# A two-layer hybrid trunk: mixers traced in small woven steps, and one block transpose per RWKV level spread on GpSimd

## The chip, the cores and the metric

One Trainium2 chip, one core. The metric is the device time of one execution in microseconds (us), the median over runs of the kernel.

## What is computed

A two-layer decoder trunk on 256 tokens of width 1024, in float32. A layer runs three mixers on the normed input h, gates and sums them, projects the sum, and then runs a dense FFN (layer 0) or a top-2-of-8 expert layer (layer 1):

```python
for l in range(DEPTH):
    mod = silu(c) @ ada_w[l] + ada_b[l]
    h = rms_norm(x, norm_mix[l]) * (1 + sc_m) + sh_m
    proj = h @ w_in[l]
    y_rw, v_first = rwkv7_mixer(...)   # S = S*w + (S a) b + v k, y = S r, per head
    y_ssd = ssd_mixer(...)             # conv, chunked state-space scan, gated norm
    y_fox = fox_mixer(...)             # causal softmax with forget gates
    merged = g_rw*(y_rw @ proj_rw[l]) + g_ssd*(y_ssd @ proj_ssd[l]) + g_fox*(y_fox @ proj_fox[l])
    x = x + g_m * (merged @ w_out[l])
    x = x + g_f * (FFN or experts)(h')
```

The RWKV recurrence is done in chunks of 128 tokens, for which a triangular 128 x 128 matrix per head has to be inverted.

## The kernel before

Every large product is made from halves: `split_part` (L148 to L158) rounds a piece of raw weights to float32r on ScalarE (L156, `hi`) and subtracts that from the raw piece on VectorE (L157, `lo`), and `mm3` (L125) multiplies hi by hi, hi by lo and lo by hi. The text calls each such TensorE instruction with 256 columns a product; a split of 128 x 512 feeds 12 of them (4 k-tiles x 3). Raw weights come in pieces of up to 1 MB through a ring of 3 buffers, loaded on SP's queue (`load_raw`). `project_cols` projects up to 256 columns of `w_in` at a time (48 products for 256 columns), `project_rows` does the same with h as weights, `gates` and `merge` project the branch gates and the branch outputs, and `mod_next` loads and sums a piece of the next modulation.

The mixers of one layer are written as generators: `rwkv_half` (two halves of four heads, tokens r0, r1), `ssd_group` (four groups, s0 to s3), `fox_half` (f0, f1), `gates` (G) and `merge` (m0 to m2). The list `ORDER` says in which order their pieces, which run from one `yield` to the next, are traced. A half of RWKV has four pieces: the projections; the decays and the matrices `mats`; the inversion; the states. A scheduler then orders each engine's instructions by the order of tracing and by what it takes to be ready; each engine runs its own list strictly in order. Merging in `ORDER` comes at the end: RWKV, SSD, FoX.

The inversion goes over levels 0 to 5 for two chunks (ch) of 128 tokens. In a level GpSimd masks the matrices (`pool.tensor_tensor`, L629, into `am`), TensorE multiplies four 32-row blocks with `tls` (L631), VectorE transposes each 32 x 128 block of the result into the diagonal blocks of `bds` (L654, four per chunk and level), TensorE multiplies by `bds` (L658), VectorE adds (L661), TensorE transposes the sum (L131) and ScalarE copies it out as `c` (L671), from which the next level starts. `bds` is zeroed once per half by GpSimd (L637). Tiles of 128 x 512 come from a ring `u` of `NUNIT` = 15, tiles `c` from a ring of `NCOMP` = 6.

The rest of the program is not touched: the first norm, `project_out`, the FFN and the experts are traced as before.

Of the kernel before, what the change touches and what calls it, by code (L numbers as in the profile page):

```python
# [36 lines left out]
NUNIT, NSSD, NSPLIT, NRAW, NB8 = 15, 7, 5, 3, 4  # L37
NMOE, NSM = 5, 7
NPOOL = 4
NCOMP = 6  # L40
# [10 lines left out]
ORDER = [  # L51
    (
        "rw r0 r0 mo r0 r0 fx sd s0 s0 s0 s1 s1 s1 r1 r1 r1 r0 s2 mo s2 s2 f0 r1 r1 s3 mo G f0 mo G s3 s3 G "
        "f0 G m0 f1 m0 f1 m0 md md m1 md m0 m1 m1 md f1 md md md m1 m2 gm m2 md m2 m2"
    ).split(),
    (
        "rw r0 r0 mo r0 sd s0 s0 r0 r0 s0 s1 mo s1 s1 s2 r1 r1 G r1 s2 fx r1 G s2 r1 G s3 s3 mo f0 f0 s3 G m0 "
        "f0 m0 mo m0 m0 f1 md f1 m1 m1 md md md gm m1 md m1 f1 m2 m2 m2 md md md m2"
    ).split(),
# [4 lines left out]
def trunk(  # L64
# [312 lines left out]
    def stationary(raw, n, evac):  # L377

        ps = dbank()
        for q in range(0, n, P):  # L380
            m = min(P, n - q)
            o = ps[:m, q * 2:q * 2 + T]
            accumulate(o, raw[:, :, q:q + m], (hh, hl))
            evac(q // P, o)

    def project_cols(wsrc, c0, n, evac):
        for p0 in range(0, n, 256):
            w = min(256, n - p0)
# [47 lines left out]
    def stages(f):  # L436

        def start(*a):
            g = f(*a)
            return lambda: next(g, None)  # L440
        return start
# [17 lines left out]
    def rwkv(mx, l, prm, lora):  # L459
# [10 lines left out]
        project_cols(w_in[l], 1536, 288, lambda i, ps: shift(wa if i == 0 else gl[:ps.shape[0], i - 1, :], ps, 12 + i))  # L470
# [14 lines left out]
        return [y[:, 0], y[:, 1]], lambda jp: stages(rwkv_half)(mx, l, prm, lora, jp, shift, wa, gl, vd, vup, y)  # L485

    def rwkv_half(mx, l, prm, lora, jp, shift, wa, gl, vd, vup, y):
# [8 lines left out]
        for dst, g in ((k, 1), (r, 0), (v, 2)):  # L496
            project_cols(w_in[l], g * RW + jp * 256, 256, lambda i, ps: shift(dst[:, i, :], ps, 4 * g + 2 * jp + i))
# [37 lines left out]


# [19 lines left out]


# [17 lines left out]


# [4 lines left out]


# [5 lines left out]
        act.activation(vrow, ps, AF.Copy)  # L588
# [909 lines left out]
```

## Time and profile before

| what | value |
|---|---|
| median of 3 runs | 2234.21 us (2226.03 to 2235.48) |
| profiled execution | 2224.52 us, span 2222.8 us |
| TensorE (PE) busy, its weight loads (PEld) | 2115.0 us (95%), 1811.2 us (81%) |
| VectorE (DVE) | 1798.8 us (81%) |
| ScalarE (ACT) | 1386.1 us (62%) |
| GpSimd (POOL) | 152.1 us (7%) |

The span falls into the first norm (to about 35 us), the mixers of layer 0 (to 478 us), the output projection and the FFN (to 722 us, with the second norm), the mixers of layer 1 (to 1171 us) and the experts. In the page's 40 slices GpSimd is busy in the mixers alone, and DMA is below a half of its share there, while it is at nine tenths in the experts.

### The profile page before, as it was taken

Reading aid. Unit: us, or ns where it says so; the run is one execution under the profiler, and the core shown is the slowest. Engines: PE = TensorE matmul, PEld = TensorE weight load, DVE = VectorE, ACT = ScalarE, POOL = GpSimd, SP = SyncE. Lnnn points to the kernel's source line nnn. Section 1 sums busy time; section 2 is a strip of 40 time slices with the busy share of each in tenths; the row PEclk is TensorE's granted clock in tenths of the full one; section 3 lists DMA queues with packets and bytes.
Section 4 is the critical chain, followed back from the end, with each engine's and each line's share of the span. In section 5 each row is a group of like instructions: output and inputs, shape, how many; then the busy total and the mean of one; then the engine's idle time right before and its main releaser. Section 6 shows DMA issues by size and latency. Waiting matters only on the chain.

```text
span 2222.8 us, 35724 instructions
## 1 busy us (share of the span) xinstructions
PE 2115.0 (95%) x13489; PEld 1811.2 (81%) x13489; DVE 1798.8 (81%) x2822; ACT 1386.1 (62%) x2204; POOL 152.1 (7%) x180
## 2 busy tenths in 40 slices
PE   7899899999998889989998999999999999999998
PEld 4777789998997877868998788888888887888776
DVE  4977776777776797756768999999999989999887
ACT  3454455555454545434555877878878777878775
POOL 2211200000000031211002000000000000000000
PEclk9999999999999998988998999999999999999999
DMA  8423254667884533414556999999999999999994
GB/s 304 128 83 95 77 172 156 213 198 259 294 286 137 145 108 93 138 53 130 184 176 251 337 362 359 324 368 367 374 337 352 355 362 336 342 364 368 336 363 151
DMA packets 316101, 546.68 MB, mean 246 GB/s; under 512 B 11952, under 2 KB 143536, under 8 KB 315920
## 3 DMA queue, kind: packets, MB, share of 16 engines
q1 hardware_dynamic: 315920, 544.31, 71.1%
q8 instruction: 108, 1.77, 0.3%
q14 instruction: 73, 0.60, 0.1%
HBM read 543.22 MB, written 1.05 MB: 245 GB/s over the span
## 4 chain that ended last, share of the span: by engine, by line
PE 79%; DVE 13%; issue 3%; ACT 2%; DMA 2%; POOL 0%; SPq 0%; DVEq 0%; ACTq 0%; POOLq 0%
PE pd L122 37%; PE pm L122 33%; PE ps L122 7%; DVE lo L157 5%; PE pm L131 1%; DVE u L654 1%; DMA araw<-in_ada_w_dram 1%; PE ps L131 1%; ACT hi L156 1%; DMA b<-in_ada_w_dram 1%; DVE cu L802 1%; DVE xr L1257 1%; DVE u L225 0%; DMA raw<-in_moe_w_gu_dram 0%; DVE b L612 0%
## 5 line engine op out<-in xcount | busy, mean ns | idle before, releaser
L156 ACT ACTIVATE hi<-raw 128x1024 fp32r<-128x1024 f32 (+2 forms) x1201 | 1027.7, 870 | 522.4 <-PE pd L122 277.0
L157 DVE TENSOR_TENSOR lo<-raw,hi 128x1024 fp32r<-128x1024 f32 (+2 forms) x1197 | 1154.6, 990 | 211.6 <-ACT hi L156 189.8
L122 PE MATMUL pd<-hh,hi 128*128 128x256 f32 (+2 forms) x1208 | 352.7, 293 | 15.3 <-ACT hh L362 3.9
L122 PE MATMUL pd<-hh,lo 128*128 128x256 f32 (+2 forms) x1208 | 346.5, 287 | 0.0
L122 PE MATMUL pd<-hl,hi 128*128 128x256 f32 (+2 forms) x1208 | 345.7, 286 | 0.3
L122 PE MATMUL pm<-lo,hh 128*128 128x512 f32 x672 | 266.7, 397 | 3.0 <-DVE lo L157 2.8
L122 PE MATMUL pm<-hi,hh 128*128 128x512 f32 x672 | 266.9, 397 | 0.1
L122 PE MATMUL pm<-hi,hl 128*128 128x512 f32 x672 | 263.0, 392 | 0.0
L122 PEld LDWEIGHTS pd<-hh,hi 128*128 128x128 f32 (+2 forms) x1208 | 231.9, 192 | 28.3 <-issue 5.6
L122 PEld LDWEIGHTS pd<-hh,lo 128*128 128x128 f32 (+2 forms) x1208 | 231.5, 192 | 6.1 <-issue 3.9
L122 PEld LDWEIGHTS pd<-hl,hi 128*128 128x128 f32 (+2 forms) x1208 | 232.7, 193 | 4.3 <-issue 2.3
L122 PE MATMUL pd<-lo,hi 128*128 128x512 f32 x448 | 174.7, 390 | 0.0
L122 PE MATMUL pd<-hi,hi 128*128 128x512 f32 x448 | 170.9, 391 | 0.1
L122 PE MATMUL pd<-hi,lo 128*128 128x512 f32 x448 | 167.8, 389 | 0.0
L122 PEld LDWEIGHTS pm<-lo,hh 128*128 128x128 f32 x672 | 126.8, 189 | 32.1 <-DVE lo L157 5.5
L122 PEld LDWEIGHTS pm<-hi,hh 128*128 128x128 f32 x672 | 126.5, 188 | 29.3 <-ACT hi L156 1.4
L122 PEld LDWEIGHTS pm<-hi,hl 128*128 128x128 f32 x672 | 126.7, 189 | 26.5
L122 PE MATMUL pm<-hi,more 128*128 128x512 f32 x448 | 142.1, 392 | 0.0
L122 PEld LDWEIGHTS pd<-hi,hi 128*128 128x128 f32 x448 | 84.1, 188 | 18.4 <-ACT hi L405 0.5
L122 PEld LDWEIGHTS pd<-hi,lo 128*128 128x128 f32 x448 | 84.1, 188 | 17.8
L122 PEld LDWEIGHTS pd<-lo,hi 128*128 128x128 f32 x448 | 84.1, 188 | 17.6
L122 PEld LDWEIGHTS pm<-hi,more 128*128 128x128 f32 x448 | 84.1, 188 | 17.5 <-ACT hi L156 0.3
(423 smaller groups left out, 3467.0 us busy)
## 6 DMA issues: line engine op xcount, KB each, us to landing
raw<-in_moe_w_gu_dram SPq DMA_DIRECT2D x224, 1024.0 KB, 7.0
raw<-in_moe_w_down_dram SPq DMA_DIRECT2D x110, 1024.0 KB, 6.8
raw<-in_w_in_dram SPq DMA_DIRECT2D x66, 1024.0 KB, 5.4
araw<-in_ada_w_dram SPq DMA_DIRECT2D x68, 512.0 KB, 4.3
raw<-in_ffn_w_gu_dram SPq DMA_DIRECT2D x22, 1024.0 KB, 6.8
raw<-in_ffn_w_down_dram SPq DMA_DIRECT2D x11, 1024.0 KB, 6.5
raw<-in_w_in_dram SPq DMA_DIRECT2D x16, 512.0 KB, 5.1
raw<-in_proj_ssd_dram SPq DMA_DIRECT2D x8, 1024.0 KB, 5.2
```

Source lines behind the costliest of these rows:

```text
L122: pe.matmul(o, lhsT, rhs, start=start, stop=stop)
L131: pe.transpose(o, i, ident[:n, :n])
L156: act.activation(hi, raw, AF.Copy)
L157: minus.tensor_sub(lo, raw, hi.bitcast(F32))
L654: dve.transpose(blk(bds[ch], q)[:, odd, bcol(q)], by4(blk(pz, q))[:, odd, :])
L802: dve.scalar_tensor_tensor(cu[:, s:T], ps[:, 0:T - s], pph[:, w:w + 1], cu[:, s:T], op0=ALU.mult, op1=ALU.add)
L1257: dve.tensor_add(xr[:, t, hs], xr[:, t, hs], po)
```

## The change

- `ORDER` becomes a list of segments. A segment holds up to three streams, whose steps are woven evenly: step i of n stands at (i + 0.5) / n. `STEPS` is the number of steps of each stream (45 for a half of RWKV, 14 for an SSD group).
- Many `yield`s are added, so that a step is one 128-column projection, one half of a level, one part of a softmax. Both layers have one order.
- SSD's gates (G) are computed first and SSD is merged first (`ma`), beside FoX; RWKV (`mb`) and FoX (`mc`) follow.
- In each level one VectorE transpose takes the whole 128 x 128 result into a tile `c`, and GpSimd multiplies it, repeated four times, by a block-diagonal mask `bmask` into `bds`. The zeroing of `bds` goes.
- `NUNIT` 15 to 14, `NCOMP` 6 to 8. Pieces of the modulation are all loaded as in `mo`; the deep form `md` is no longer used in the mixers.

```diff
-NUNIT, NSSD, NSPLIT, NRAW, NB8 = 15, 7, 5, 3, 4
+NUNIT, NSSD, NSPLIT, NRAW, NB8 = 14, 7, 5, 3, 4
-NCOMP = 6
+NCOMP = 8
-ORDER = [
-    (
-        "rw r0 r0 mo r0 r0 fx sd s0 s0 s0 s1 s1 s1 r1 r1 r1 r0 s2 mo s2 s2 f0 r1 r1 s3 mo G f0 mo G s3 s3 G "
-        "f0 G m0 f1 m0 f1 m0 md md m1 md m0 m1 m1 md f1 md md md m1 m2 gm m2 md m2 m2"
-    ).split(),
...
+STEPS = dict(r=45, s=14, f=21, G=9, ma=9, mb=17, mc=17)
+ORDER = 2 * [
+    [
+        ["rw"], ["r0:7"], ["sd"],
+        ["r0:25", "s0. s1:4", "mo"],
+        ["r0:8", "s1. s2:4", "mo"],
+        ["r0.", "r1:7 s2:2", "mo"],
+        ["r1:25", "s2. s3. G:4", "mo"],
+        ["r1:8", "G. ma:4", "mo"],
+        ["r1.", "fx f0:8 ma:2"],
+        ["f0.", "ma. f1:7", "mo mo"],
+        ["f1.", "mb:8", "mo mo"],
+        ["mb.", "mo"], ["gm"], ["mc."],
+    ],
 ]
...
         for ch in range(2):
             bds[ch] = unit(mx, 4, P)
-            pool.memset(bds[ch], 0.0)
...
             for ch in range(2):
                 pz = level(ch, lv, tls[ch])
-                for q in range(4):
-                    dve.transpose(blk(bds[ch], q)[:, odd, bcol(q)], by4(blk(pz, q))[:, odd, :])
+                ct = sq128()
+                dve.transpose(ct, pz)
+                pool.tensor_tensor(bds[ch].rearrange("p n (q c) -> p n q c", q=4)[:, odd],
+                                   by4(ct)[:, odd, :].unsqueeze(2).broadcast_to([P, len(range(4)[odd]), 4, 32]),
+                                   by4(bmask).unsqueeze(1).broadcast_to([P, len(range(4)[odd]), 4, 32]), op=ALU.mult)
+            yield
...
+                    b = (1, 0, 2)["abc".index(step[1])]
+                    return merge(mx, l, prm, b, made["merged"], made["y"][b], (proj_rw, proj_ssd, proj_fox)[b][l], (4, 8, 4)[b], b == 1)
...
+            for segment in ORDER[l]:
+                streams = [steps(stream) for stream in segment]
+                for _, _, name in sorted(((i + 0.5) / len(x), k, name) for k, x in enumerate(streams) for i, name in enumerate(x)):
+                    assert take(name), (name, counts, taken)
```

The order on ScalarE in layer 0, second half of RWKV, at the copies of the levels (`c<-pm`, two per level, one for each chunk); `hi<-raw` is the rounding that feeds 12 products, `s` and `ysh` are SSD's. Before, from the second copy of level 1 to the first of level 4:

```order
L671 ACTIVATE c_2418<-pm_2416 128x128
L847 ACTIVATE s_2848<-s_2848 128x512
L847 ACTIVATE s_2849<-s_2849 128x512
L671 ACTIVATE c_2458<-pm_2456 128x128
L671 ACTIVATE c_2462<-pm_2460 128x128
L671 ACTIVATE c_2502<-pm_2500 128x128
L671 ACTIVATE c_2506<-pm_2504 128x128
L872 ACTIVATE s_2969<-s_2878 128x512
L671 ACTIVATE c_2546<-pm_2544 128x128
```

and now, from the second copy of level 2 to the first of level 3 alone:

```order
L694 ACTIVATE c_3046<-pm_3044 128x128
L163 ACTIVATE hi_3695<-raw_3630 128x512
L163 ACTIVATE hi_3727<-raw_3724 128x512
L1000 ACTIVATE b_716_3233<-pd_3513,pph_234 128x256
L163 ACTIVATE hi_3743<-raw_3724 128x512
L163 ACTIVATE hi_3773<-raw_3724 128x512
L163 ACTIVATE hi_3789<-raw_3724 128x512
L694 ACTIVATE c_3159<-pm_3157 128x128
```

Where copies of two levels stood one behind the other, five splits of the SSD gates now stand between them.

The order on GpSimd in the same half: `u<-b,ztm` is the mask product of a level (`ztm_340` is level 2, `ztm_351` level 3, `ztm_362` level 4, `ztm_375` level 5; the two `b` are the two chunks), `u<-c,bmask` the new spread (`u_2886` for chunk 0, `u_2889` for chunk 1), `sm` a power for a norm:

```order
L648 TENSOR_TENSOR u_3087<-b_588_2730,ztm_351 128x512
L648 TENSOR_TENSOR u_3097<-b_607_2831,ztm_351 128x512
L648 TENSOR_TENSOR u_3172<-b_588_2730,ztm_362 128x512
L674 TENSOR_TENSOR u_2886<-c_2997,bmask 128x512
L674 TENSOR_TENSOR u_2889<-c_3007,bmask 128x512
L141 TENSOR_TENSOR sm_3193<-sm_3192,mhalf 128x2
L648 TENSOR_TENSOR u_3182<-b_607_2831,ztm_362 128x512
L648 TENSOR_TENSOR u_3270<-b_588_2730,ztm_375 128x512
L674 TENSOR_TENSOR u_2886<-c_3094,bmask 128x512
L674 TENSOR_TENSOR u_2889<-c_3104,bmask 128x512
```

Before, GpSimd had the mask products alone here; now the spread of level 2 stands behind the mask products of levels 3 and 4, and that of level 3 behind those of levels 4 and 5 and behind a power that waits for SSD.

## Rows read from the trace of the kernel before

**Rows 1.** Windows, stretches of both mixers: length, busy us by engine, PEclk, DMA share, GB/s

```profile
core 0: us, PE busy (x) PEld busy (x) DVE busy (x) ACT busy (x) POOL busy (x), PEclk, DMA share, GB/s
44.60:71.50 26.90, 26.10 (x209) 23.93 (x209) 24.08 (x91) 17.34 (x41) 0.00 (x0) 1.00 0.42 114
71.50:253.30 181.80, 158.23 (x1378) 133.00 (x1382) 142.36 (x326) 79.50 (x194) 46.77 (x55) 0.93 0.31 91
253.30:478.20 224.90, 222.80 (x1868) 205.49 (x1864) 158.07 (x310) 125.98 (x275) 11.15 (x10) 0.99 0.56 176
722.30:763.00 40.70, 38.55 (x313) 35.55 (x314) 29.81 (x93) 26.01 (x56) 0.00 (x0) 1.00 0.55 154
763.00:970.00 207.00, 184.64 (x1560) 155.25 (x1563) 168.24 (x367) 97.42 (x234) 49.45 (x53) 0.93 0.36 106
970.00:1171.00 201.00, 195.72 (x1604) 177.94 (x1596) 127.50 (x247) 105.24 (x226) 12.46 (x14) 0.94 0.47 147
```

**Rows 2.** Windows, the four stretches of levels 1 to 4, in order of time

```profile
108.00:140.00 32.00, 26.60 (x289) 21.04 (x284) 26.04 (x72) 13.62 (x39) 8.27 (x12) 0.89 0.35 113
224.40:253.30 28.90, 23.59 (x252) 17.64 (x248) 21.39 (x61) 10.20 (x33) 12.15 (x17) 0.89 0.15 38
795.60:833.20 37.60, 33.95 (x341) 28.09 (x341) 33.85 (x85) 15.56 (x35) 9.35 (x13) 0.86 0.29 86
945.40:970.00 24.60, 18.35 (x207) 13.91 (x211) 19.15 (x56) 8.37 (x29) 7.20 (x10) 0.93 0.15 45
```

**Rows 3.** Timeline of PE (start, length, idle before): products after a wait, and in a dense stretch

```profile
79.77 0.51 PE L122 MATMUL pd<-hh,hi 128*128 128x256 f32 x1 [2.96 <-DVE vfirst L468]
80.08 0.42 PE L122 MATMUL pd<-hl,hi 128*128 128x256 f32 x1
80.29 0.41 PE L122 MATMUL pd<-hh,lo 128*128 128x256 f32 x1
80.50 0.41 PE L122 MATMUL pd<-hh,hi 128*128 128x256 f32 x1
...
83.28 0.30 PE L122 MATMUL pd<-hl,hi 128*128 128x256 f32 x1
...
476.73 0.28 PE L122 MATMUL pd<-hi,hh 128*128 128x256 f32 x1
476.84 0.28 PE L122 MATMUL pd<-lo,hh 128*128 128x256 f32 x1
476.95 0.28 PE L122 MATMUL ps<-hi,hh 128*128 128x256 f32 x1
```

**Rows 4.** Lines by form: busy us, mean ns of one, idle before

```profile
L157 DVE TENSOR_TENSOR lo<-raw,hi 128x512 fp32r<-128x512 f32 x524 | 364.6, 703 | 150.2 <-ACT hi L156 142.8 <-PE pd L122 3.3 <-PE pm L131 0.5
L629 POOL TENSOR_TENSOR u<-b,ztm 128x512 f32<-128x512 f32 x48 | 59.9, 1265 | 104.5 <-PE pm L122 63.2 <-DVE b L612 41.2
L654 DVE STREAM_TRANSPOSE u<-pm 32x128 f32<-32x128 f32 x128 | 39.9, 312 | 14.1 <-PE pm L122 11.7
L654 DVE STREAM_TRANSPOSE u<-pm 32x64 f32<-32x64 f32 x32 | 7.9, 246 | 1.6 <-PE pm L122 1.0
```

**Rows 5.** Timeline of POOL in layer 0, mask products

```profile
97.47 8.06 POOL L629 TENSOR_TENSOR u<-b,ztm 128x512 f32<-128x512 f32 x6 [3.35 <-DVE b L612]
108.81 2.27 POOL L629 TENSOR_TENSOR u<-b,ztm 128x512 f32<-128x512 f32 x2 [3.28 <-PE pm L122]
```

**Rows 6.** Timeline of DVE beside them

```profile
97.67 1.50 DVE L225 SCALAR_TENSOR_TENSOR u<-araw,silc,u 128x512 f32<-128x512 f32 x1
99.10 0.72 DVE L612 COPY_PREDICATED b<-mmask,pm 128x512 f32<-128x512 uint8 x1
...
101.54 1.65 DVE L225 SCALAR_TENSOR_TENSOR u<-araw,silc,u 128x512 f32<-128x512 f32 x1
103.12 1.39 DVE L805 SCALAR_TENSOR_TENSOR xb<-zt,cu 128x256 f32<-128x256 f32 x1
104.42 1.65 DVE L157 TENSOR_TENSOR lo<-raw,hi 128x512 fp32r<-128x512 f32 x1
106.00 0.74 DVE L225 SCALAR_TENSOR_TENSOR u<-araw,silc,u 128x512 f32<-128x512 f32 x1
...
109.06 2.60 DVE L654 STREAM_TRANSPOSE u<-pm 32x128 f32<-32x128 f32 x8
...
113.55 0.43 DVE L805 SCALAR_TENSOR_TENSOR xb<-zt,cu 128x256 f32<-128x256 f32 x1 [0.59 <-ACT zt L804]
```

**Rows 7.** Waits, 71.5 to 253.3 us: total, times, longest

```profile
ACT hi L156 <- PE pd L122: 41.5, 32, 6.1
POOL u L629 <- PE pm L122: 31.2, 9, 6.9
...
PE pm L122 <- DVE u L654: 8.4, 9, 1.7
```

More of the change, by code (lines that the diff above doesn't have):

```diff
@@ L388, in project_cols @@
             w = min(256, n - p0)
-            stationary(load_raw(rows(wsrc, 0, D, c0 + p0, w), KD, w), w, lambda i, ps: evac(p0 // P + i, ps))
+            yield from stationary(load_raw(rows(wsrc, 0, D, c0 + p0, w), KD, w), w, lambda i, ps, i0=p0 // P: evac(i0 + i, ps))
     def project_rows(wsrc, c0, y):
@@ L434, in pair, with whole @@
         return keep(a, [P, KD, T], F32R), keep(b, [P, KD, T], F32R)
[L436 to L441, printed above, removed]
+    def whole(g):
+        while True:
+            try:
+                next(g)
+            except StopIteration as e:
+                return e.value
     def hblock(hb):
@@ L1003, in project_out @@
             qs = slice((q % 2) * 256, (q % 2) * 256 + 256)
-            ps = project_rows(w_out[l], q * 256, (mh, ml))
+            ps = whole(project_rows(w_out[l], q * 256, (mh, ml)))
             for t in range(2):
@@ L1391, in trunk, with steps @@
                     gm = keep("vfirst", [P, 2, 512]) if l == 1 else mx("u2", [P, 2, 512])
[L1392 to L1405 removed]
+                    made["gm"] = [gm[:, 0], gm[:, 1]]
+                    mod_row(lambda: unit(mx, 4, P), l, 2, 0.5, made["gm"])
+                else:
+                    if token not in run:
+                        run[token] = part(token)
+                    if run[token] is None:
+                        return False
+                    counts[token] = counts.get(token, 0) + 1
+                    if next(run[token], done) is done:
+                        run[token] = None
+                return True
+            taken = {}
+            def steps(stream):
+                names = []
+                for word in stream.split():
+                    name, _, n = word.rstrip(".").partition(":")
+                    n = STEPS[name if name in STEPS else name[0]] - taken.get(name, 0) if word[-1] == "." else int(n or 1)
+                    taken[name] = taken.get(name, 0) + n
+                    names += [name] * n
+                return names
+            for segment in ORDER[l]:
+                streams = [steps(stream) for stream in segment]
+                for _, _, name in sorted(((i + 0.5) / len(x), k, name) for k, x in enumerate(streams) for i, name in enumerate(x)):
+                    assert take(name), (name, counts, taken)
+            assert not any(run.values()), [k for k in run if run[k]]
+            merged, gm = made["merged"], made["gm"]
             dump(f"merged{l}", merged)
```

110 lines of the change are left out of this document (64 added, 46 removed).

## The prediction, made before the change was run

> **What bounds the kernel now.** I read the page's busy shares first, then the windows by stage, then the order, and then the lines, waits and timelines of the mixers. TensorE is 95% busy over the span, so only what PE loses counts, and the order says where to look: outside the mixers the instructions of FFN and experts stand as they did. The two mixers take 44.6 to 478.2 us and 722.3 to 1171 us; I split each at the first key norm of RWKV's half 0 and at the last level of half 1 [rows 1]. The middle stretch is where PE is not fed: in 71.5 to 253.3 us it is busy 158.2 of 181.8 us at a mean granted clock of 0.93, in 763 to 970 us 184.6 of 207 us at 0.93. The merges behind are dense: 222.8 of 224.9 us in layer 0. So products stand in a queue at the end of the mixer while PE idles in its middle. The worst part is the levels: four of them take 24.6 to 37.6 us, and PE is busy 74 to 90% of it, with small matmuls [rows 2]. A level is a chain PE, DVE, PE, DVE, PE, ACT, so it cannot hurry; what can be done is to put products between.
>
> The clock makes a gap dearer than it is. After PE had waited 2.96 us, products followed each other at 0.213 us (80.29 to 80.50), down to 83.28; in a dense stretch at 0.113 us [rows 3]. That is 1.2 against 2.4 GHz. A mean clock of 0.93 over 181.8 us is 0.14 x 181.8 = 25 us at the lower level, or 12.7 us lost; over 207 us it is 14.5 us lost.
>
> DVE is busy 142.4 of 181.8 us and 168.2 of 207 us in the same two stretches [rows 1], that is 78 and 81%. Any product moved there brings DVE work along, so DVE is the engine to watch.
>
> **The change, part by part.**
>
> *Products moved forward.* I counted 256-column products on PE in both orders. Between the last level of half 1 and the end of the merges there were 1350 in layer 0 and are now 934; in layer 1 1121 and 912. So 416 and 209 leave the tail. The tail gives back what an instruction takes there: 224.9 us / 1868 = 0.120 us each, 50.1 us in layer 0; 201 / 1604 = 0.125 us, 26.2 us in layer 1 [rows 1].
>
> They arrive in the middle stretch at 0.113 us each [rows 3]: 47.1 and 23.7 us. What can take them up is PE's idle time and what the clock loses there. Layer 0: 23.6 + 12.7 = 36.3 us. Layer 1: 22.4 + 14.5 = 36.9 us. Not all of it is won, since steps still wait for their chain now and then. I take 85%, 31 us, in both. Why so much: in the tail, where products and FoX's softmax chain stand mixed, PE is busy for 99% [rows 1], and between two levels of half 1 in layer 0 the order has now 62 to 81 products (7 to 9 us of PE) where it had 0 to 48. The ends are none and all of it. Layer 0: 47.1 - 31 = 16 us longer in the middle, 50 us shorter in the tail, **-34 us**. Layer 1: 23.7 us fit into 31 us, the middle stays as long as it is, **-26 us**.
>
> *The tail of layer 1* runs at a clock of 0.94, so 12 us are lost to it, and 5.3 us are idle [rows 1]. It is the states of half 1 with too little beside them. SSD's merge is traced there now. I take **-5 us**, with the ends 0 and -17.
>
> *VectorE.* 160 transposes of 32 rows go: 39.9 + 7.9 = 47.8 us [rows 4]. 40 of 128 x 128 come. The trace has none with 128 partitions; if its time goes by columns it is 0.31 us, if by blocks 4 x 0.31 = 1.25 us. I take 0.31 us, since the 32 x 64 form with half the columns takes 0.246 us against 0.312 us [rows 4], so columns count. 40 x 0.31 = 12.4 us; DVE is relieved of 35.4 us, with an end of nothing at 1.25 us. A split feeds 12 products, so the moved ones bring 625 / 12 = 52 subtractions of 0.70 us [rows 4] into the middle: 36.6 us. DVE's work there stays what it was, near 80%. No gain of its own; it is what lets the products in.
>
> *GpSimd.* 32 spreads of 128 x 512 and 8 of half that size come. The nearest row is the mask product with the same shape and a bfloat16 mask, 1.27 us alone or crowded [rows 4], 1.14 us each in a pair [rows 5]; with 0.6 us for the small ones some 42 us over the program, on an engine at 7%. Its place in the chain matters more. Before, a level's eight transposes took 2.60 us [rows 6]. Now two transposes and two spreads overlap: 0.31 + 2.27 = 2.58 us [rows 4, 5], and one more hand-over. Nothing in the chain, then, and nothing against either sign of some tenths; 20 levels by 0.3 us would be 6 us, beside products that cover it.
>
> *GpSimd against VectorE.* While GpSimd ran six mask products from 97.47 us, VectorE's subtraction of two SBUF tiles took 1.65 us, a modulation sum 1.50 and 1.65 us (0.74 us at 106.00), L805 1.39 us (0.43 us at 113.55), but the masked copy out of PSUM 0.72 us, and the transposes from PSUM beside the pair of masks ran on at 0.32 us each [rows 5, 6]. So an instruction with two SBUF inputs waits for GpSimd's. A subtraction that meets a spread loses 1.65 - 0.69 = 0.96 us. From none to all of 40 spreads: 0 to 38 us. I take a quarter, **+9 us**: after a level's transposes DVE has work with PSUM inputs as often as subtractions, and it waits for others a fifth of the time.
> The Trainium skill, "SBUF — State Buffer", section "Who interferes with whom", speaks against this change: a VectorE instruction with two SBUF inputs contends with a GpSimd instruction that reads SBUF, and the second one blocks until the first is through. The rows above agree with it.
>
> *The rest.* Modulation: as many pieces are loaded, in four DMAs instead of eight for those that were deep; their sums stay on DVE. The raw ring is still three deep; counted in the order, from the last product on one piece to the first on the third after it there are nearly always over 5.5 us of products, before and now, about the median landing of 5.4 us that the page shows for these loads. So I cost SP's queue at nothing; without that cover a late piece costs its remaining flight. `u` with one tile fewer: GpSimd's mask products already wait 31.2 us for tiles that PE has to release [rows 7], early masks at that, so nothing.
>
> **Sum:** -34 - 26 - 5 + 9 = -56 us on the profiled execution of 2224.5 us (span 2222.8 us). That run is 9.7 us below the median of 2234.2 us, so I predict 2234.2 - 56 = **2178 us**. A measurement of this kernel tells about 0.5% (11 us) from no change.
>
> **Rivals.**
>
> *The spreads lock VectorE.* Each spread holds one subtraction for its whole length, 38 us instead of 9, in stretches where DVE is at 80% and feeds PE. For it: rows 6, where five DVE instructions in a row were held. Against it: in half of GpSimd's pairs DVE was in its transposes. Time: 2178 + 29 = 2207 us. Chance 0.12. This is what the section "Who interferes with whom" of the Trainium skill's "SBUF — State Buffer" would make of it if orders always met.
>
> *Woven work only moves the wait.* PE stays as badly fed in the middle as it was, and what leaves the tail makes the middle longer by the same. For it: ACT's roundings waited 41.5 us for products to release their tiles [rows 7], so PE was at times the one behind. Layer 0: 47.1 - 50.1, layer 1: 23.7 - 26.2, no gain in the tail: -5.5, +9 us for the lock, 2238 us. Chance 0.11.
>
> *Slower: late spreads stop PE.* PE's list is strict. A multiplication by `bds` whose spread is late stops every product behind it. GpSimd's list is strict too, and a spread stands behind mask products of later levels, which wait for `u` tiles, and behind a power that waits for SSD. If in each of 20 levels two masks come between (2.27 us [rows 5]), PE loses that, and then some 16 products at the lower clock, 16 x 0.1 = 1.6 us [rows 3]: 20 x 3.9 = 77 us against 56 us won, +21 us: 2255 us. It turns the sign from 2.8 us lost per level. Against it: the masks need only the matrices of the half and a tile, and in the trace they were issued while the chain was elsewhere; PE waited only 8.4 us in nine waits for transposes [rows 7]. Chance 0.08.
>
> *All of it fits.* Idle time and clock losses of both middles and the tail of layer 1 are won whole, the lock costs nothing: layer 0 -50.1 + 47.1 - 36.3 = -39, layer 1 -26.2 + 23.7 - 36.9 - 17 = -56: 2139 us; with PE's small matmuls also better hidden some 10 us less. Chance 0.11. That the order is not what the source says is ruled out, as the counts above are of the built lists.
>
> **How the numbers follow.** Forecast 0.58 (its own range 2150 to 2206: share taken up 70 to 100%, lock 0 to 20 us), lock 0.12, moved wait 0.11, late spreads 0.08, all fits 0.11. The range leaves out the late spreads and a part of the best case: 2130 to 2238. Faster by over 0.5%: forecast, lock and all fits, 0.81, less a little for forecasts that end near the bound: 0.79. The same: the moved wait and that little, 0.12. Slower: 0.09.
>
> **What would show it.** Right: 934 and 912 products behind the last level; PE's idle time in the middles below 10 us and the clock there above 0.96; the middle of layer 0 about 198 us long, of layer 1 207 us, the tails 175 and 170 us; FFN and experts within 1 us; transposes x40 at 0.31 us; spreads at 1.15 to 1.7 us. A mean of L157's 128 x 512 form above 0.75 us would be the lock. PE waiting for `u` from GpSimd for over 20 us would be the late spreads. Wrong: middles that grow by over 45 us, or DVE over 90% busy in them with PE idle.

## The result, and the profile after

The changed kernel takes 2249.54 us (median of 5 runs, 2245.16 to 2250.75) against 2231.21 us of the kernel before on the same chip: a ratio of 1.0079, 95% interval 1.0058 to 1.0101. It is slower by 0.8%, some 18 us, where 56 us less were forecast.

The page's line of busy shares of the changed kernel (profiled execution 2250.75 us), then its windows of the two middles and the two tails, as in [rows 1]:

```profile
PE 2140.6 (95%) x13489; PEld 1833.8 (82%) x13489; DVE 1779.6 (79%) x2703; ACT 1382.3 (61%) x2204; POOL 210.8 (9%) x212
```

```profile
core 0: us, PE busy (x) PEld busy (x) DVE busy (x) ACT busy (x) POOL busy (x), PEclk, DMA share, GB/s
73.70:328.80 255.10, 225.62 (x1886) 197.66 (x1886) 192.90 (x376) 115.82 (x269) 77.75 (x72) 0.91 0.41 125
328.80:503.60 174.80, 170.97 (x1359) 154.37 (x1359) 102.96 (x202) 90.27 (x200) 13.04 (x11) 0.93 0.44 136
791.30:1028.20 236.90, 218.32 (x1829) 187.32 (x1828) 185.91 (x367) 112.05 (x261) 78.65 (x72) 0.93 0.42 126
1028.20:1200.20 172.00, 168.32 (x1333) 152.29 (x1330) 96.21 (x186) 89.14 (x199) 12.65 (x10) 0.93 0.40 123
```

The tails are what was forecast (175 and 170 us). The middles are not: layer 0's went from 181.8 to 255.1 us, layer 1's from 207 to 236.9 us. Products arrived there as counted: in the traces, 256-column products that start in the middle went from 627 to 1046 in layer 0 and from 774 to 983 in layer 1, 419 and 209 more. At 0.113 us they are 47.3 and 23.6 us; the middles grew by 73.3 and 29.9 us. So nothing was taken up by idle PE. Idle time plus clock loss (the share of the clock that was not granted, times the length) of layer 0's middle even rose, from 36.3 us to 29.5 + 0.09 x 255.1 = 52 us; layer 1's stayed at 18.6 + 0.07 x 236.9 = 35 us.

The four windows together are 24.1 us longer than before. PE's idle time in them went from 53.3 to 55.6 us, its clock loss from 41.5 to 63.8 us. So nearly all of the loss is PE at work under a lower granted clock; over the program it has as many instructions as before, is idle for 2249.0 - 2140.6 = 108.4 us against 2222.8 - 2115.0 = 107.8 us, and is busy 25.6 us longer.

That layer 0's tail met its forecast is in part luck. 509 instructions left it (1868 to 1359), small matmuls beside the 416 products that were counted, and its clock fell from 0.99 to 0.93, which is some 10 us more of clock loss. Some 90 and 60 small matmuls came into the middles with the products, which the forecast had not counted either.

The four stretches of levels 1 to 4 of the changed kernel, same columns, which answer to [rows 2]:

```profile
113.40:165.50 52.10, 43.40 (x417) 37.49 (x417) 38.22 (x75) 26.11 (x69) 27.45 (x27) 0.90 0.28 82
284.00:328.80 44.80, 44.80 (x465) 40.26 (x465) 33.92 (x56) 22.89 (x51) 27.83 (x26) 1.00 0.46 142
826.20:872.80 46.60, 41.91 (x417) 35.37 (x416) 37.38 (x74) 21.62 (x52) 26.76 (x24) 0.93 0.38 113
983.70:1028.20 44.50, 43.68 (x462) 38.79 (x460) 31.32 (x52) 19.18 (x39) 27.00 (x26) 1.00 0.46 141
```

In both layers the levels of half 1 became what the change is after: PE busy for 98 to 100% of the time at full clock. In half 0 of layer 0 they lose 8.7 us to idle time and run at 0.90.

The larger loss lies elsewhere. Ahead of the levels of each half stands a stretch from the key norm to the first level, with RWKV's elementwise work on VectorE. These four stretches, before and then in the changed kernel, same columns:

```profile
71.50:108.40 36.90, 30.72 (x219) 26.43 (x220) 33.94 (x61) 12.21 (x24) 13.13 (x12) 0.91 0.43 123
195.10:224.80 29.70, 26.17 (x206) 21.82 (x206) 27.22 (x56) 11.75 (x24) 9.80 (x10) 1.00 0.37 107
762.90:796.00 33.10, 27.07 (x188) 21.56 (x188) 32.69 (x62) 13.80 (x35) 13.57 (x12) 1.00 0.46 136
908.10:945.80 37.70, 35.46 (x271) 30.55 (x270) 28.98 (x59) 15.53 (x31) 12.85 (x13) 1.00 0.42 122
```

```profile
73.70:113.40 39.70, 32.88 (x230) 28.98 (x230) 33.22 (x67) 13.15 (x27) 6.58 (x6) 0.87 0.46 138
241.10:284.00 42.90, 32.31 (x227) 27.43 (x226) 33.25 (x68) 12.74 (x29) 7.37 (x8) 0.88 0.37 115
791.30:826.20 34.90, 29.83 (x189) 24.66 (x189) 29.38 (x60) 13.95 (x36) 6.43 (x6) 0.85 0.33 98
946.00:983.70 37.70, 35.03 (x235) 29.47 (x235) 35.35 (x71) 17.12 (x42) 7.24 (x6) 0.91 0.42 130
```

PE's idle time plus clock loss by kind of stretch, both layers together, worked out from such windows (e9 is the kernel below in which both side costs are mended; with clocks of two digits the sums are good to some 1.5 us):

| us | before | changed | e9 |
|---|---|---|---|
| ahead of the levels | 21.3 | 44.1 | 24.2 |
| levels of half 0 | 17.7 | 21.9 | 15.0 |
| levels of half 1 | 16.0 | 0.8 | 0.7 |
| between the halves | 17.8 | 22.1 | 12.2 |

The lines of the changed kernel by form, over the program (L673 is the transpose, L674 the spread, L648 the mask product, L164 the subtraction), with L164 in the middle of layer 0 last, and behind them the subtraction in that middle before:

```profile
L673 DVE STREAM_TRANSPOSE c<-pm 128x128 f32<-128x128 f32 x40 | 11.4, 304 | 8.1 <-PE pm L129 8.0
L674 POOL TENSOR_TENSOR u<-c,bmask 128x512 f32<-128x512 f32 x32 | 45.2, 1427 | 67.3 <-DVE c L673 54.7 <-ACT s L872 12.6
L674 POOL TENSOR_TENSOR u<-c,bmask 128x256 f32<-128x256 f32 x8 | 7.5, 952 | 5.7 <-DVE c L673 5.7
...
L164 DVE TENSOR_TENSOR lo<-raw,hi 128x512 fp32r<-128x512 f32 x524 | 382.3, 737 | 174.7 <-ACT hi L163 170.5 <-ACT s L877 0.9 <-PE pm L138 0.8
...
L164 DVE TENSOR_TENSOR lo<-raw,hi 128x512 fp32r<-128x512 f32 x87 | 71.6, 831 | 34.0 <-ACT hi L163 32.9 <-ACT s L877 0.9
```

```profile
L157 DVE TENSOR_TENSOR lo<-raw,hi 128x512 fp32r<-128x512 f32 x51 | 37.2, 731 | 15.7 <-ACT hi L156 14.6 <-PE pd L122 0.5 <-ACT s L830 0.3
```

The timelines of GpSimd and VectorE in half 0 of layer 0, and of GpSimd in half 1, show two things about the spread:

```profile
120.92 9.05 POOL L648 TENSOR_TENSOR u<-b,ztm 128x512 f32<-128x512 f32 x6
130.82 2.63 POOL L674 TENSOR_TENSOR u<-c,bmask 128x512 f32<-128x512 f32 x2 [0.85 <-DVE c L673]
```

```profile
125.75 1.64 DVE L164 TENSOR_TENSOR lo<-raw,hi 128x512 fp32r<-128x512 f32 x1
127.31 1.64 DVE L878 TENSOR_TENSOR s<-s,s 128x512 f32<-128x512 f32 x1
128.87 1.64 DVE L164 TENSOR_TENSOR lo<-raw,hi 128x512 fp32r<-128x512 f32 x1
130.44 0.30 DVE L673 STREAM_TRANSPOSE c<-pm 128x128 f32<-128x128 f32 x1
130.67 0.64 DVE L164 TENSOR_TENSOR lo<-raw,hi 128x512 fp32r<-128x512 f32 x1
```

```profile
308.21 2.75 POOL L648 TENSOR_TENSOR u<-b,ztm 128x512 f32<-128x512 f32 x2 [3.55 <-PE pm L129]
310.92 3.20 POOL L674 TENSOR_TENSOR u<-c,bmask 128x512 f32<-128x512 f32 x2
```

At 120.92 six masks run in one go, two of level 2, whose result the spread needs, and four of levels 3 and 4, which it doesn't; VectorE's instructions beside them take 1.64 us instead of 0.64, and the transpose that the chain waits for stands behind three of them on VectorE's list. At 308.21 two masks of later levels, which had themselves waited 3.55 us for a `u` tile from PE, stand ahead of two spreads; the spreads follow without a gap, so they had been ready. From the end of its transpose to its start, a spread waits 1.31 us on the mean of 40, 52.5 us in all (worked out from the two engines' timelines); 33.0 us of that are the second of a pair, which also waits for the first.

The last suspect is in the waits of the same middle (total, times, longest) and in the chain of work that ended last (start, length):

```profile
DVE u L232 <- DMA araw<-in_ada_w_dram: 5.6, 4, 2.9
...
PE pm L129 <- POOL u L674: 4.7, 3, 2.3
```

```profile
97.71 5.84 DMA araw<-in_ada_w_dram
```

VectorE stands in its list for pieces of the modulation, which I had costed at nothing.

### The profile page after: what moved, and what is told of

Its sections match the earlier page's. It is cut to its first block, busy times and chain, and to the rows that moved or that the text cites. A ratio compares the mean times of both kernels' runs of the same rounds, so it can differ in the third digit from the quotient of the medians.

```text
span 2249.0 us, 35555 instructions
## 1 busy us (share of the span) xinstructions
PE 2140.6 (95%) x13489; PEld 1833.8 (82%) x13489; DVE 1779.6 (79%) x2703; ACT 1382.3 (61%) x2204; POOL 210.8 (9%) x212
## 4 chain that ended last, share of the span: by engine, by line
PE 82%; DVE 10%; DMA 3%; issue 2%; ACT 2%; POOL 1%; SPq 0%; DVEq 0%; ACTq 0%; POOLq 0%
PE pd L129 38%; PE pm L129 34%; PE ps L129 7%; DVE lo L164 4%; DMA araw<-in_ada_w_dram 2%; PE pm L138 2%; PE ps L138 1%; ACT hi L163 1%; DVE cu L831 1%; DMA xr<-in_x_dram 1%; DVE u L232 1%; DVE xr L1293 0%; DVE b L631 0%; SPq L252 0%; POOL sm L141 0%
## 5 line engine op out<-in xcount | busy, mean ns | idle before, releaser
L164 DVE TENSOR_TENSOR lo<-raw,hi 128x1024 fp32r<-128x1024 f32 (+2 forms) x1197 | 1170.8, 1006 | 232.0 <-ACT hi L163 215.2
L129 PE MATMUL pd<-hh,hi 128*128 128x256 f32 (+2 forms) x1208 | 359.7, 299 | 20.9 <-DVE cu L831 9.8
L129 PE MATMUL pd<-hl,hi 128*128 128x256 f32 (+2 forms) x1208 | 350.7, 291 | 0.3
L129 PEld LDWEIGHTS pd<-hh,hi 128*128 128x128 f32 (+2 forms) x1208 | 238.0, 197 | 38.8 <-issue 15.2
L129 PEld LDWEIGHTS pd<-hl,hi 128*128 128x128 f32 (+2 forms) x1208 | 237.6, 197 | 4.9 <-issue 2.6
L129 PEld LDWEIGHTS pd<-hh,lo 128*128 128x128 f32 (+2 forms) x1208 | 236.5, 196 | 5.9 <-issue 3.4
L129 PEld LDWEIGHTS pd<-hi,hi 128*128 128x128 f32 x448 | 84.1, 188 | 18.2 <-ACT hi L415 0.3
L129 PEld LDWEIGHTS pd<-hi,lo 128*128 128x128 f32 x448 | 84.1, 188 | 17.8 <-DVE lo L416 0.2
```

Of the source, the lines that this page charges most:

```text
L129: pe.matmul(o, lhsT, rhs, start=start, stop=stop)
L164: minus.tensor_sub(lo, raw, hi.bitcast(F32))
```

## The experiments

All ratios are to the kernel before on the same chip, with their 95% intervals. The lengths are windows between the same marks as above, each of one profiled execution (e1's windows are those of e15, the same kernel).

| kernel | ratio | middle, tail L0 | middle, tail L1 |
|---|---|---|---|
| before | 1 | 181.8, 224.9 | 207.0, 201.0 |
| changed | 1.0079 [1.0058, 1.0101] | 255.1, 174.8 | 236.9, 172.0 |
| e1, e15: woven, four transposes | 1.012 [1.0098, 1.0143] | 249.2, 180.1 | 236.6, 178.7 |
| e2: old order, GpSimd spread | 1.010 [1.0081, 1.0118] | 198.9, 221.6 | 220.1, 198.0 |
| e3: woven, VectorE spread | 0.9993 [0.998, 1.0006] | 232.5, 180.1 | 226.5, 175.3 |
| e4: changed, pieces moved | 1.0032 [1.0017, 1.0046] | 236.6, 187.4 | 229.9, 178.2 |
| e5: changed, spreads ahead of masks | 0.9982 [0.9961, 1.0003] | 237.1, 175.8 | 231.5, 173.8 |
| e6: e3 and idle spreads on GpSimd | 1.0011 [0.9998, 1.0025] | 246.6, 172.7 | 239.3, 168.3 |
| e7: e3 and e4 | 0.9929 [0.9912, 0.9946] | 220.0, 183.2 | 219.0, 185.5 |
| e8: old order, VectorE spread | 1.0063 [1.0043, 1.0082] | 191.1, 227.8 | 210.3, 203.6 |
| e9: e5 and e4 | 0.9939 [0.9925, 0.9954] | 228.2, 183.2 | 213.9, 180.3 |
| e10: e7, gates elsewhere | 1.0123 [1.0105, 1.0141] | 240.0, 204.2 | 216.2, 185.2 |
| e11: e1 and e4 | 0.9955 [0.9938, 0.9971] | 218.2, 185.1 | 216.3, 182.4 |
| e12: e9, gates elsewhere | 1.0132 [1.0113, 1.0152] | - | - |

Two things limit what the lengths say. The clock moves them: the tail of layer 0 has the same work in e3 and e6, and the two rows differ by 7.4 us, at 0.93 and 0.97:

```profile
305.80:485.90 180.10, 176.07 (x1395) 159.23 (x1396) 105.39 (x208) 91.68 (x203) 10.31 (x9) 0.93 0.45 139
320.30:493.00 172.70, 169.48 (x1396) 154.49 (x1397) 106.50 (x208) 92.15 (x203) 11.66 (x12) 0.97 0.47 146
```

And a middle ends with RWKV's chain, not with a fixed number of products. In layer 0 it holds 1046 in the changed kernel, 1015 in e5, 1009 in e3 and e6, 963 in e4, 1002 in e7, 1023 in e9, 966 in e11 and 972 in e15; in layer 1 983, 941, 892 and 919, 918, and 891 in the last four. A shorter middle can hold fewer products, and the tail has them then.

The three theories at first: S, the spread on GpSimd costs; O, the woven order itself costs, since chain steps stand behind filler on VectorE's list; M, VectorE's waits for the modulation cost.

**e1, order alone.**

```diff
-                ct = sq128()
-                dve.transpose(ct, pz)
-                pool.tensor_tensor(bds[ch]... , op=ALU.mult)
+                for q in range(4):
+                    dve.transpose(blk(bds[ch], q)[:, odd, bcol(q)], by4(blk(pz, q))[:, odd, :])
```

> The changed kernel with its woven order, but with the four VectorE transposes of 32 x 128 per chunk and level and the zeroing of bds put back; GpSimd spreads nothing. The changed kernel stood at 1.008 of the one before. Theory S (the spread costs: GpSimd's 1.4 us instruction stands in the chain, and VectorE's 128 x 512 subtractions went from 0.73 to 0.83 us beside GpSimd): 0.99 to 1.00 of before, the middle of layer 0 back by 20 us or more. Theory O (the order costs: chain steps stand behind the filler's subtractions on VectorE): 1.010 to 1.025 of before, since VectorE gets some 35 us of transposes back in stretches where it is the engine waited for. Theory M (VectorE stands in its list for the modulation's loads): about as O, 1.01 or more.

1.012: the four transposes put back make the woven kernel no faster.

**e2, spread alone**, in the old order, with `ct`, `pool.tensor_tensor` and a mask `[P, 4]` repeated over 32 columns in place of the four transposes.

> The kernel before with its own order, where only the inversion is changed: one VectorE transpose and GpSimd's spread by a mask (here of one column for each block of 32, repeated), bds not zeroed, rings u and c of 15 and 6 as before. Theory S: slower than before, 1.005 to 1.015, the level stretches of layer 0 (32 and 29 us) longer by 3 us or more each. Theory O: 0.990 to 1.000 of before; the mean of the subtraction L157 in the middles under 0.76 us. Theory M: 0.99 to 1.00 of before.

1.010, as S said; the levels of layer 0 took 45.3 and 39.4 us instead of 31.9 and 28.9. e1 alone spoke for O or M, e2 for S: neither theory does it alone.

**e3, the same spread on VectorE.**

```diff
-                pool.tensor_tensor(bds[ch]...
+                dve.tensor_tensor(bds[ch]...
```

> The changed kernel with the same spread issued on VectorE instead of GpSimd. Theory S: 0.99 to 1.00 of before, if a VectorE multiplication of 128 x 512 takes about 0.7 us, in spite of some 28 us more on VectorE. Theory O: 1.010 to 1.020 of before, VectorE being the engine with the queue. Theory M: about 1.01.

0.9993: 0.9% better than the changed kernel, though VectorE has 33.6 + 3.2 us more to do. Theory O, which expected 1.010 to 1.020 here, is not tenable beside this.

**e4, the modulation's pieces moved out of RWKV's segments.**

```diff
-        ["r0:25", "s0. s1:4", "mo"],
+        ["r0:25", "s0. s1:4"],
...
-        ["f0.", "ma. f1:7", "mo mo"],
+        ["f0.", "ma. f1:7", "mo mo mo"],
```

> The changed kernel with the pieces of the modulation (mo) taken out of the five segments of RWKV and put into the segments of FoX, SSD's merge and RWKV's merge, as many in all. Theory M: 0.990 to 0.998 of before; the middle of layer 0 back from 255 to 230 us or less, the tails 3 to 10 us longer. Theories S and O: the middle of layer 0 shorter by the 25 us of VectorE sums that leave it at most, the tail longer by as much; 1.004 to 1.010 of before.

1.0032, between the two expectations: the middles lost 18.5 and 7.0 us, the tails gained 12.6 and 6.2 us; 83 and 65 products went into the tails with the sums. A real cost, and not the largest.

**e5, spreads ahead of masks.** GpSimd's list of the changed kernel in half 0 of layer 0, and of e5 (`bmask` rows are the spreads, `ztm_340` to `ztm_362` the masks of levels 2 to 4, the spreads those of level 2; the lines moved from L648 to L652 and from L674 to L680):

```
46 L648 TENSOR_TENSOR u_1314<-b_232_1080,ztm_340 128x512
47 L648 TENSOR_TENSOR u_1324<-b_238_1109,ztm_340 128x512
48 L648 TENSOR_TENSOR u_1363<-b_232_1080,ztm_351 128x512
49 L648 TENSOR_TENSOR u_1373<-b_238_1109,ztm_351 128x512
50 L648 TENSOR_TENSOR u_1461<-b_232_1080,ztm_362 128x512
51 L648 TENSOR_TENSOR u_1471<-b_238_1109,ztm_362 128x512
52 L674 TENSOR_TENSOR u_1165<-c_1321,bmask 128x512
53 L674 TENSOR_TENSOR u_1168<-c_1331,bmask 128x512
```

```
46 L652 TENSOR_TENSOR u_1314<-b_232_1080,ztm_340 128x512
47 L652 TENSOR_TENSOR u_1324<-b_238_1109,ztm_340 128x512
48 L680 TENSOR_TENSOR u_1165<-c_1321,bmask 128x512
49 L680 TENSOR_TENSOR u_1168<-c_1331,bmask 128x512
```

```diff
-            pool.tensor_tensor(am, mbs[ch][:, :, 0, :], bc4(ztmask[lv]), op=ALU.mult)
+            if lv > 1:
+                with tc.issue_after(after[0]):
+                    pool.tensor_tensor(am, mbs[ch][:, :, 0, :], bc4(ztmask[lv]), op=ALU.mult)
+            else:
+                pool.tensor_tensor(am, mbs[ch][:, :, 0, :], bc4(ztmask[lv]), op=ALU.mult)
...
+            after[0] = spread.ins
```

> The changed kernel in which GpSimd's masks of a level (L648, 1.4 us each) are ordered behind the spreads of the level before; up to six masks for later levels stood ahead of a waiting spread on GpSimd's list. The spread on VectorE instead of GpSimd has been measured: 0.9993 of before against 1.008. Theory Q (what the spread costs is its place on GpSimd's list, behind the masks): 0.998 to 1.002 of before, the level stretches of layer 0 (52 and 45 us) shorter by 5 us or more each. Theory K (what it costs is VectorE's slowing beside GpSimd, six operations of 1.6 us in a row for 0.7): 1.005 to 1.010, as the changed kernel, since as much GpSimd work lies beside VectorE.

0.9982, as theory Q said of the ratio: the same instructions on the same engines, in another order on GpSimd's list, take back 1.0%. The Trainium skill, "PSUM — Partial Sum Buffer", section "Engine vs sequencer instructions", calls the queues of ScalarE, VectorE and GpSimd strictly first in, first out; the trace agrees, with spreads behind masks as the list has them. GpSimd's timeline of e5 in half 1 of layer 0:

```profile
293.29 2.82 POOL L680 TENSOR_TENSOR u<-c,bmask 128x512 f32<-128x512 f32 x2 [3.58 <-DVE c L679]
296.07 3.18 POOL L652 TENSOR_TENSOR u<-b,ztm 128x512 f32<-128x512 f32 x2
302.24 2.75 POOL L680 TENSOR_TENSOR u<-c,bmask 128x512 f32<-128x512 f32 x2 [2.99 <-DVE c L679]
```

GpSimd now waits for the transposes, and the masks run behind. A spread waits 0.67 us from its transpose (26.9 us over 40), most of that the second of a pair behind the first. The four level stretches went from 188.0 us to 159 us (from the ACT marks 112.8, 154.1, 270.0, 310.1, 812.4, 846.7, 958.6 and 1002.1 us); those of layer 0 by 10.8 and 4.7 us, the second just short of the 5 us expected. That is not the gain: PE's busy time in them fell by 25 of the 29 us, since fewer products stand there. What got better is idle time and clock loss in layer 0, from 13.9 to 5.8 us in the levels of half 0 and from 28.2 to 17.4 us between them and those of half 1; layer 1 has 36 us without the edge and 38 us with it, though its spreads wait 14.6 us less.

That the place on the list is what costs does not rest on e5 alone. The same edge takes 0.93% off e4 (that is e9), and e3, which leaves the masks early and only takes the spread off GpSimd's list, takes 0.86% off the changed kernel (the slowing that this saves too is priced by e6 at some 4 us). How a late spread turns into this much is not traced: from e4 to e9 the spreads' wait falls by 8 us (34.2 to 26.0 us) and the time by some 21 us. The edit also breaks up bursts like that of six masks; which part of the 1.0% that is was not taken apart.

**e6, the slowing beside GpSimd alone**: e3 with a GpSimd product by zero of the same shape at levels 1 to 4.

```diff
+                if lv < 5:
+                    pool.tensor_tensor(tms[ch]..., by4(ct)..., zero4..., op=ALU.mult)
```

> The changed kernel with the spread on VectorE, and a multiplication of the same shape on GpSimd beside it (by zero, into tm, which is zero anyway), at levels 1 to 4: 32 of 1.4 us on which no engine waits at once. Theory K (slowing beside GpSimd): 1.004 or more of before, the mean of the subtraction L164 in the middle of layer 0 back from 0.72 to 0.78 us or more. Theory Q (place on the list): 0.998 to 1.002, as without it, but for masks that come late.

1.0011, 0.0018 above e3 with intervals that overlap: some 4 us for 32 instructions. In the middle of layer 0, e3 first, e6 second:

```profile
L164 DVE TENSOR_TENSOR lo<-raw,hi 128x512 fp32r<-128x512 f32 x85 | 60.4, 719 | 16.4 <-ACT hi L163 15.3 <-PE pd L129 0.6
```

```profile
L164 DVE TENSOR_TENSOR lo<-raw,hi 128x512 fp32r<-128x512 f32 x85 | 67.3, 800 | 21.0 <-ACT hi L163 21.0
```

The slowing is there, 0.72 to 0.80 us as K expected; its price is small, and these runs don't tell it from nothing. In one execution of each the middles of e6 are 14.1 and 12.8 us longer than e3's and the tails 7.4 and 7.0 us shorter; the ratio, over 12 executions of each, is the better guide. e5 (792 ns) and the fastest kernel, e7 (796 ns), have the same mean.

**e7, VectorE's spread and the pieces moved.**

> The changed kernel with the spread on VectorE and the pieces of the modulation moved out of RWKV's segments: the two edits that gave -0.9% and -0.5% alone. If the two costs are separate: 0.993 to 0.996 of before. If both are one thing (VectorE's list is too long in the middles): 0.997 to 1.000.

0.9929: the costs are separate. At 2213.85 us against 2229.08 us of the kernel before on the same chip it is faster than both kernels.

**e8, the old order with VectorE's spread.**

> The kernel before with its own order and the new spread issued on VectorE (one transpose and one multiplication for four transposes of 32 x 128). Against the woven order with the same spread (0.9993) it shows what the order alone does. Theory O (the woven order costs, since chain steps stand behind filler): 0.988 to 0.997 of before. If the woven order costs nothing of itself: 0.999 to 1.003.

1.0063, on neither expectation: the woven order is 0.7% better than the old one with the same spread. But in the old order's memory the ring `c` stayed at 6, with two tiles more in use per level, in e2 as well; so neither of them is a clean price of the spread in the old order.

**e9, spreads first and the pieces moved.**

> The changed kernel with the spread left on GpSimd but the masks of a level ordered behind it, and the pieces of the modulation moved out of RWKV's segments: the edits that brought 1.008 to 0.9982 and to 1.0032 alone. Separate costs: 0.992 to 0.996 of before, as the spread on VectorE with the same move (0.9929). One cost seen twice: 0.997 to 1.000.

0.9939, as expected of separate costs; it matters little which engine spreads, once the spread isn't late. Its middles:

```profile
70.10:298.30 228.20, 212.52 (x1848) 186.28 (x1849) 169.74 (x340) 114.57 (x267) 75.35 (x70) 0.96 0.34 100
...
769.10:983.00 213.90, 195.75 (x1721) 168.28 (x1720) 159.66 (x323) 107.07 (x254) 71.01 (x68) 0.96 0.31 93
```

**e10, another filler.** The windows of e7 from the first key norm to the first level, half 1, both layers, and PE's and VectorE's timelines in the second of them:

```profile
219.00:256.20 37.20, 32.88 (x230) 28.54 (x231) 30.20 (x59) 16.05 (x40) 13.79 (x12) 0.86 0.24 73
...
905.50:942.60 37.10, 28.85 (x201) 23.79 (x200) 28.39 (x58) 11.89 (x28) 12.14 (x11) 0.86 0.25 76
```

```profile
916.47 1.22 PE L129 MATMUL pm<-u,bones 128*128 128x256 f32 x2 [7.23 <-DVE u L589]
```

```profile
911.67 0.42 DVE L577 TENSOR_SCALAR u<-u 128x512 f32<-128x512 f32 x1
912.01 0.69 DVE L416 TENSOR_TENSOR ysl<-s,ysh 128x512 fp32r<-128x512 f32 x1
912.61 0.87 DVE L831 SCALAR_TENSOR_TENSOR cu<-pd,pph,cu 128x254 f32<-128x254 f32 x2
913.39 0.68 DVE L579 TENSOR_TENSOR u<-u,u 128x512 f32<-128x512 f32 x1
```

PE's next instruction needs RWKV's elementwise results, VectorE works through them without a gap with SSD's convolutions between, and behind PE's waiting instruction nothing can pass.

```diff
-        ["r0:25", "s0. s1:4"],
+        ["r0:25", "s0:2 G:5 s0:11"],
...
-        ["r1:25", "s2. s3. G:4"],
+        ["r1:25", "s2:2 G. s2. s3:9"],
```

> The fastest so far (spread on VectorE, pieces of the modulation moved, 0.9929) with another filler beside RWKV's elementwise steps: five and four steps of the gates in the place of as many steps of SSD, whose steps go where the gates were. There the trace shows TensorE waiting 10.5 us in layer 1 for u of L589, VectorE busy with RWKV's elementwise work and SSD's convolutions. Theory V (VectorE is the bound of that stretch, a filler that loads it less lets TensorE run): 0.988 to 0.992 of before, the stretch from the first key norm to the first level shorter by 3 us or more in each half. If the stretch is bound by RWKV's own chain: 0.992 to 0.995.

1.0123, on neither expectation: worse by 1.9%. The stretch in question grew from 40.3 to 50.1 us in half 0 of layer 0 and from 37.2 to 39.8 us in half 1, and the tail of layer 0 from 183.2 to 204.2 us. In e10, the stretch ahead of the levels in half 1 of layer 0, and those levels:

```profile
233.00:272.80 39.80, 37.92 (x311) 33.79 (x310) 35.49 (x65) 18.90 (x42) 12.24 (x10) 1.00 0.45 133
272.80:311.20 38.40, 30.98 (x298) 26.12 (x294) 30.20 (x64) 15.45 (x38) 9.71 (x14) 0.82 0.18 56
```

There the gates did fill PE: 311 instructions instead of 230, at full clock instead of 0.86. But the levels that they had filled in e7 (37.10 us, PE busy throughout at full clock) now leave PE idle for 7.4 us at 0.82. The filler was moved, not won. Why half 0's stretch got longer stays open.

**e11, order alone, pieces moved** (the edits of e1 and e4).

> The changed kernel's woven order with the pieces of the modulation moved, and the four VectorE transposes of 32 x 128 with the zeroing of bds put back: the order alone, without the spread. With the four transposes and the pieces in RWKV's segments it stood at 1.012. If the waits for the modulation's loads are a cost of their own: 1.005 to 1.008. If weaving needs VectorE's time that the one transpose frees (35 us): 1.008 to 1.013.

0.9955, better than either expectation: the woven order with all pieces in the tails is a gain of 0.45%, and the pieces in RWKV's segments turn it into a loss of 1.2%. The kernel before had 24 of its 88 sums in the middles (8 and 16), the changed one 64, e11 none; so a part of the gain may be those 24. The old order with its pieces moved was not run, nor the new rings of 14 and 8 tiles by themselves.

**e12, e9 with e10's filler.**

> The spread on GpSimd ahead of the masks, the pieces of the modulation moved, and the gates beside RWKV's elementwise steps, all at once. If the three gains add up: 0.988 to 0.992 of before. If relief of VectorE by GpSimd is eaten by slowing beside it: 0.992 to 0.996.

1.0132, on neither: the filler undoes it here too.

**e13 and e14, why the pieces cost.** Wait taken away; then seven of eight sums too.

```diff
     def mod_sum(sc, raws, key):
+        if sc is mx:
+            raws = [xr[:, kt // 4, 0:512] for kt in range(KD)]
```

> The changed kernel in which the mixers' sums of the modulation read x, which has long been in SBUF, instead of the loaded pieces; the loads are issued as before and nothing reads them. The modulation of the later blocks is wrong by that; the number and size of the instructions are the same. The changed kernel stood at 1.008, with the pieces moved at 1.0032. Theory W (VectorE stands in its list for the loads): 1.001 to 1.005 of before. Theory A (the sums themselves, 0.8 us each, are VectorE's work in stretches where it is the engine waited for): 1.006 to 1.009.

> The changed kernel in which a piece of the modulation is summed in the mixers by one VectorE instruction instead of eight, from x instead of the loaded piece; seven of eight sums are left out, the loads stay. Theory W: as without the wait, 1.001 to 1.005 of before, but for the sums that leave the tail too. Theory A: 0.996 to 1.002, clearly below the kernel with all the sums and no wait.

The ratios (1.4707 and 1.4613) say nothing here: with other modulations the part behind the mixers took 2080 us instead of 1049. The mixers can be compared. Their middles, e13 first, e14 second:

```profile
70.10:319.90 249.80, 221.30 (x1887) 194.19 (x1887) 192.33 (x376) 115.86 (x269) 77.11 (x72) 0.92 0.41 125
786.50:1019.60 233.10, 216.19 (x1828) 186.53 (x1828) 191.35 (x371) 112.66 (x262) 78.64 (x72) 0.94 0.32 95
```

```profile
70.10:306.20 236.10, 214.86 (x1857) 187.48 (x1857) 174.19 (x346) 114.05 (x266) 75.52 (x72) 0.93 0.41 127
774.30:1004.20 229.90, 208.44 (x1814) 180.73 (x1813) 172.63 (x339) 111.43 (x260) 76.92 (x72) 0.94 0.31 93
```

Without the waits the two middles are 5.3 and 3.8 us shorter, about what VectorE waited for `araw` (5.6 and 4.7 us), with as many products in them; without the sums 13.7 and 3.2 us more, with 30 and 14 products fewer, some 5 us. So of 26 us theory W has a third, theory A between 12 and 17 us, in one execution of each. Moving the pieces (e4) took 25.5 us off the middles, and the tails took 18.8 us of that back.

**e15, the trace of e1.**

> The woven order with the four VectorE transposes and the pieces of the modulation in RWKV's segments once more, for its trace (1.012 of before; 0.9955 with the pieces moved). Theory A: VectorE is busy over 0.8 of the middle of layer 0, and that middle is longer than the 218 us of the kernel with the pieces moved by more than the 22 us of its sums. Theory W: VectorE waits for the modulation's loads by 10 us or more there.

VectorE is busy 191.1 of 249.2 us there (0.77, not over 0.8) and waits 2.0 us for the loads. That middle is 31 us longer than e11's, with nearly as many products (972 and 966): more than the sums, which take 23.5 us there, as A had it, and against W. What the other 7 us are, and why the pieces cost 1.65% with the four transposes and 0.43 to 0.64% where the spread was mended, stays open.

## Why the prediction was wrong

- **Products moved forward: right in number, wrong in what takes them up.** Counts and tails (50.1 and 29.0 us shorter, forecast 50.1 and 31) held, the first tail in part by luck. The -5 us for the tail of layer 1 did not come in its own terms: idle time and clock loss there went from 17.3 to 15.7 us, at a clock of 0.93. The step that failed is "85%" of 73.2 us of idle time and clock loss. The changed kernel took up nothing of it, and its middles have 87.6 us; the sign set for being wrong, a middle that grows by over 45 us, showed in layer 0 with 73.3 us. With both side costs mended, e9 has 15.7 + 0.04 x 228.2 = 24.8 us left in layer 0's middle and 18.2 + 0.04 x 213.9 = 26.7 us in layer 1's: 21.7 of 73.2 us taken up, 30%. e11, without a GpSimd spread, gets 14.1 us, 19%. Both are one execution each, and layer 1's middles hold 117 products more than before there, not 209. In the forecast's own terms the middles should have grown by 16 us and nothing; in e9 they grew by 46.4 and 6.9 us. What was taken up in e9 goes by place: of 16.0 us in half 1's levels nearly all, of 17.7 us in half 0's levels 2.7 us, of 21.3 us ahead of the levels nothing. The support for 85% was a tail where SSD's and FoX's products have little chain beside them, and half 1's levels, which did fill up. The rest of the middle was averaged in.
- **GpSimd's place in the chain: the largest side cost, put at nothing.** "Nothing in the chain" compared 2.60 us of transposes with 2.58 us of transpose and spread as if GpSimd were free at that moment. Its list had masks ahead. The rival of late spreads named just this mechanism and 2255 us, and got 0.08; e5 gives it 0.97%, 22 us. That its time came within 6 us is luck: it had 77 us of stops against 56 us won, and the runs have 22 us against 14 us. "Early masks were issued while the chain was elsewhere" was true while nothing of the chain stood on GpSimd. The sign I had set for it, PE waiting over 20 us for `u` from GpSimd, did not show (4.7 us in layer 0's middle). That a late level shows as waits of PE for other things behind it is argued, not shown; what the rows show is clock loss. The wait from transpose to spread was the better sign of the mechanism, though not of its price.
- **Modulation at nothing: wrong.** 0.43 to 0.64% where the spread was mended (e5 to e9, e3 to e7), 1.65% with the four transposes (e1 to e11), for all 64 sums in the middles; 40 of them came there by the change, so its own share is less. I had counted DMAs and left the sums "on DVE"; 64 of 88 stood in tails, where DVE is busy 59% of the time in layer 0 of the changed kernel, and 40 of those came into middles where it is at 76 to 78%.
- **GpSimd against VectorE: +9 us was right in sign, its size stays open.** The mean of the subtraction in layer 0's middle went from 0.73 to 0.83 us; over the program it went from 0.70 [rows 4] to 0.74 us, under the 0.75 us set as a sign; the 524 subtractions took 17.7 us more in all. e6 prices 32 spreads at some 4 us, not apart from nothing.
- **Transposes**: 40 of 0.304 us, as taken. **VectorE's "no gain of its own"**: e11 to e7 makes one VectorE multiplication and one transpose for four transposes worth 0.26%, with intervals that overlap.
- **The sum**, by the same ratios, so that it has to close. 2231 us with 22 us for late spreads and 10 us for the pieces, less 14 us that remain as the gain (e9, 0.9939), is 2249 us. Forecast were 65 us of gain and 9 us for the lock. "Woven work only moves the wait" (0.11) came nearest in effect for the order, the late spreads in time.

## What to carry to other kernels

When a step of a chain moves to a nearly idle engine, read that engine's list at that place: work issued early because it was off the chain is then ahead of the chain, and one ordering edge can be worth the whole change. Don't put one share on all idle time: here half 1's levels took the filler up and the stretches ahead of the levels did not, so split the share by stretch, and count clock loss beside idle time, since nearly all of this loss was clock. Keep side work of the engine that feeds the filler (here the modulation's sums on VectorE) for stretches where it is not waited for.

## What the runs showed of the hardware

- A VectorE transpose of 128 x 128 took 0.304 us, a fourth of such a tile (32 x 128) 0.312 us [rows 4]: four in one cost what one did.
- GpSimd is slowed beside VectorE too: of the changed kernel's 8 half-size spreads, mean 0.95 us, one took 0.68 us (at 1028.67) and the next, which began with a subtraction of VectorE at 1029.30, 1.24 us. VectorE's own spread of 128 x 512 in e3 took 1.07 us on the mean, and 0.65 to 0.68 us where no mask ran beside it. The Trainium skill, "SBUF — State Buffer", section "Who interferes with whom", calls the port pair that the two engines share an exclusive lock, and has the order of issue decide who blocks; rows with either engine lengthened agree. e6 gives what 32 more GpSimd products are worth here, some 4 us with nothing not excluded.
